# A hybrid decoder step on one core: side work placed by an estimated clock of each engine, weights split two pieces ahead

## The chip, the cores and the metric

The kernel runs on one core of a Trainium2 chip. The metric is the device time of one execution in microseconds; the median of several runs is given. In the text PE is TensorE, DVE is VectorE, ACT is ScalarE, POOL is GpSimd and SP is SyncE, which here only issues DMAs.

## What is computed

One layer of a decoder for 2048 prompt tokens and 8 sample tokens (one new token each for 8 sequences with a paged cache of 4096 positions), all in float32, with a model width of 1024. Cut to what matters:

```python
mod = silu(c) @ w_ada + b_ada                 # shift, scale and gate, twice
h = rmsnorm(x, norm1_g) * (1 + scale1) + shift1
z = h @ w_in
y_a = chunk_spatial_gating(gelu(z_a), ...)    # group A, 256 columns
y_b = silu(layernorm(causal_dwconv(glu(z_b), 31 taps)))   # group B, 256 columns
y_c = attend(q, k, v, logf)                   # group C, 8 heads x 64, forgetting attention
y = concat(rms(y_a), rms(y_b), rms(y_c)) * mix_g
x = x + gate1 * (y @ w_out)
h = rmsnorm(x, norm2_g) * (1 + scale2) + shift2
up = causal_dwconv(h @ w_up, 3 taps)          # d_ff = 2816
x = x + gate2 * ((silu(up[:, :d_ff]) * up[:, d_ff:]) @ w_down)
```

The sample tokens go through the same layer with the same weights. Their attention reads 32 pages of 128 positions for keys and as many for values, per sequence, through a page table. The results are the normalized outputs, the new K, V and forget rows, and the convolution states.

## The kernel before

**Stages.** The prompt is cut into 4 chunks of 512 tokens (`NCH`, `T`), each of 4 blocks of 128 (`NB`). Phase 1 (to about 670 us) makes norm1, the product with `w_in` and what hangs on it, chunk by chunk; phase 2 (to about 1180 us) is the prompt's attention; phase 3 is `w_out`, norm2, `w_up`, the short convolution, `w_down` and the final norm. The order in phase 3 is w_out of chunks 0 and 1, then per chunk four parts, each of an `up` (6 or 4 column tiles `j`) and a `down`. The w_out of chunks 2 and 3 stands before the last `down` of the chunk ahead of it. Each large product is done three times in a reduced float32 type: both operands are split in a high and a low part (`wh`, `wl`; `hh`, `hl`; `ah`, `al`; `yh`, `yl`), and `mm3` (lines 84 to 86) multiplies high by high, low by high and high by low. There are 9792 of these triples. The program's place is counted in them below: "product n".

**Weights.** `piece()` gives out weight pieces in a fixed sequence: `raw` is loaded by SP three pieces ahead, ACT copies it to `wh`, POOL subtracts for `wl`, one piece ahead of its use.

**Side work.** All that isn't one of the large products is written as Python generators, and fixed places in the main loops step them: `next(self.side)` behind groups of products (norm_c, norm2), `advance()` and `later(gen, delay)` in phase 1 with delays counted in groups, `ada_rest` with two steps a group in chunks 1 and 2, `bg(n)` for the sample attention, which hands out `n` credits that the yielded numbers use up. Each engine executes its own instructions in the order in which the program writes them, so these places decide who waits for whom. In phase 1 the ada weights (`wada`, four tiles for each of 8 steps of `k`, twice) are loaded through ACT's queue, and norm1 of the next chunk transposes 8 tiles of `x` at a time, then `modulate` makes `hmod`, `hh` (ACT) and `hl` (DVE).

**Sample attention** (lines 1100 to 1240). Per sequence s, `logits(s)` multiplies 16 tiles `pg` (two pages of keys each) by the query `qb`, sums to `red` and scales into `S`, all on DVE. `values(s)` takes the maximum `mx` on DVE, transposes it on PE, makes `dg`, spreads it with a product of ones, exponentiates on ACT, sums `lsum` and spreads that by PE, then makes the value products: each of 16 value tiles (two pages) gives two matmuls of 32 output columns, into the 32-row strip `j = 2 * (x % 2) + i` of `po`. A last one adds the new token (`vs`). The generators of one sequence's values and the next one's logits alternate. Value tiles come from `pg` and, while `lent` is set, from the buffers `yy` of w_out's `y` (named `yv` then), never more than 3 of each held. After the last sequence, `sample_rows` makes the sample tokens' gating, convolution and norms in 8 rows, and leaves them transposed in `hsT`, which w_out of the last chunk uses: `sample_mm` takes the `raw` weights of that w_out.

**w_out of chunks 2 and 3** reads `y` by pairs: `y_of` issues a load of `yh` and one of `yl` for up to three pairs ahead, on SP. `norm_c` normalizes group C of one chunk (`wk` holds squares and factors) in four steps with counts between (`waits`).

## Time and profile before

| what | value |
|---|---|
| median of 3 runs | 3123.56 us (3122.35 to 3125.27) |
| the profiled execution | 3115.85 us |
| its span | 3113.7 us, 41614 instructions |
| granted TensorE clock, mean | 0.975 of full |
| PE busy in 0 to 60, 60 to 670, 670 to 1180, 1180 to 3113 us | 38.6, 561.6, 489.5, 1861.9 us |
| granted clock in the same | 0.94, 0.97, 0.95, 0.98 |
| DMA | 523.9 MB, mean 168 GB/s |

How to read the rows that follow. A row of a group of instructions has its line, engine and operation, the tiles (output before the arrow, inputs behind) and their shapes, a count, the busy time and the mean of one in ns, and the idle time of the engine in front of it with what ended it. A row of PE's waits names the waiting instruction, what released it, and the sum, number and longest of the waits. The profile records two entries for a plain float32 matmul of the value strips.

### The profile page before, as it was taken

The page shows a single profiled execution, that of the slowest core. Times are in us where ns is not written, and L with a number is a line of the kernel's source. Part 1 is how long each engine was busy: PE and PEld are TensorE (multiplying, and loading weights), DVE is VectorE, ACT ScalarE, POOL GpSimd, SP SyncE. Part 2 cuts the span into 40 slices and gives each one's busy share as a digit, 9 for nine tenths or more (in the row PEclk, how much of TensorE's full clock was granted, in tenths as well). Part 3 has the DMA queues.
Part 4 walks back from the last instruction along what each step waited for, and adds up shares of the span by engine and source line. Part 5 has one row for each costly group of instructions (what it writes and reads, how often), then busy time and mean ns, then how long its engine had stood idle before and what let it go on. Part 6 is the DMA issues. An engine that isn't in the chain of part 4 may idle for free. (4 is left out here: it accounts for less than half of the span.)

```text
span 3113.7 us, 41614 instructions
## 1 busy us (share of the span) xinstructions
PE 2951.6 (95%) x14352; PEld 2151.2 (69%) x14352; DVE 2087.9 (67%) x2767; ACT 1228.0 (39%) x1717; POOL 1338.4 (43%) x884
## 2 busy tenths in 40 slices
PE   7998989899999989989999999999999999999998
PEld 4776768765555547767776767777767776777775
DVE  4838384858777763986887968785958554645454
ACT  4453535233333343434335433443433433534333
POOL 3544354423333444544444444454444454344443
PEclk9999999999999979999999999999999999999999
DMA  8355756563412327766677787678866627322222
GB/s 260 108 181 171 238 174 205 150 176 80 95 44 63 99 81 281 226 209 200 200 220 236 220 246 212 206 220 284 261 185 191 177 79 235 111 82 82 82 82 78
DMA packets 443589, 523.90 MB, mean 168 GB/s; under 512 B 35111, under 2 KB 281173, under 8 KB 443362
## 3 DMA queue, kind: packets, MB, share of 16 engines
q1 hardware_dynamic: 414418, 478.25, 51.3%
q10 hardware_dynamic: 28672, 41.95, 4.0%
q8 instruction: 113, 1.85, 0.2%
q0 software_dynamic: 288, 1.05, 0.1%
q14 instruction: 98, 0.80, 0.1%
HBM read 453.08 MB, written 68.38 MB: 167 GB/s over the span
## 5 line engine op out<-in xcount | busy, mean ns | idle before, releaser
L1525 POOL TENSOR_TENSOR wl<-raw,wh 128x1024 fp32r<-128x1024 f32 x296 | 769.3, 2609 | 874.9 <-ACT wh L1524 841.9
L84 PE MATMUL acc<-hh,wh 128*128 128x512 f32 x1792 | 721.0, 403 | 3.1 <-ACT hh L451 2.1
L85 PE MATMUL acc<-hl,wh 128*128 128x512 f32 x1792 | 709.4, 396 | 1.8 <-DVE hl L452 1.3
L86 PE MATMUL acc<-hh,wl 128*128 128x512 f32 x1792 | 709.1, 396 | 0.1
L1524 ACT CAST wh<-raw 128x1024 fp32r<-128x1024 f32 x296 | 308.8, 1047 | 552.9 <-PE acc L86 163.7
L1692 DVE SCALAR_TENSOR_TENSOR uy<-ub,fw,uy 128x512 f32<-128x512 f32 x352 | 282.8, 851 | 234.0 <-ACT uy L1689 232.6
L84 PEld LDWEIGHTS acc<-hh,wh 128*128 128x128 f32 x1792 | 338.2, 189 | 127.7 <-issue 22.0
L86 PEld LDWEIGHTS acc<-hh,wl 128*128 128x128 f32 x1792 | 338.4, 189 | 81.5 <-POOL wl L1525 1.0
L85 PEld LDWEIGHTS acc<-hl,wh 128*128 128x128 f32 x1792 | 338.6, 189 | 79.4 <-DVE hl L452 2.1
L496 POOL TENSOR_TENSOR wl<-raw,wh 128x512 fp32r<-128x512 f32 (+1 forms) x160 | 240.1, 1520 | 205.8 <-ACT wh L495 168.7
L84 PE MATMUL acc<-wh,ah 128*128 128x512 f32 x752 | 310.6, 413 | 16.0 <-ACT ah L1698 11.1
L86 PE MATMUL acc<-wh,al 128*128 128x512 f32 x752 | 303.6, 404 | 1.6 <-DVE al L1699 1.6
L85 PE MATMUL acc<-wl,ah 128*128 128x512 f32 x752 | 303.1, 403 | 1.0 <-POOL wl L1525 1.0
L963 POOL TENSOR_TENSOR lsum<-lsum,pt 128x512 f32<-128x512 f32 x96 | 141.0, 1469 | 203.8 <-PE misc L965 102.5
L676 DVE SCALAR_TENSOR_TENSOR cv<-glu,convw,cv 128x512 f32<-128x512 f32 x240 | 226.0, 1004 | 0.0
L1164 DVE TENSOR_TENSOR pg<-pg,qb 128x1024 f32<-128x1024 f32 x128 | 198.4, 1552 | 36.0 <-DMA pg<-in_cache_k 32.7
L995 ACT ACTIVATE pt<-acc 128x1024 f32<-128x1024 f32 (+2 forms) x144 | 126.9, 883 | 240.0 <-PE acc L993 182.5
L84 PEld LDWEIGHTS acc<-wh,ah 128*128 128x128 f32 x752 | 145.7, 194 | 77.1 <-issue 23.9
L84 PE MATMUL acc<-wh,hh 128*128 128x256 f32 (+2 forms) x552 | 163.4, 296 | 9.2 <-DVE nm L871 7.2
L86 PEld LDWEIGHTS acc<-wh,al 128*128 128x128 f32 x752 | 145.3, 193 | 37.9 <-DVE al L1699 3.9
L869 DVE TENSOR_REDUCE nm<-acc 128x1 f32<-128x1024 f32 (+1 forms) x128 | 121.5, 950 | 71.8 <-PE acc L864 71.1
L85 PEld LDWEIGHTS acc<-wl,ah 128*128 128x128 f32 x752 | 145.8, 194 | 32.8 <-POOL wl L1525 1.4
(382 smaller groups left out, 4836.9 us busy)
## 6 DMA issues: line engine op xcount, KB each, us to landing
raw<-in_w_up SPq DMA_DIRECT2D x176, 512.0 KB
pg<-in_cache_k SPq DMA_DIRECT2D x256, 256.0 KB
raw<-in_w_down SPq DMA_DIRECT2D x88, 512.0 KB
yv<-in_cache_v SPq DMA_DIRECT2D x138, 256.0 KB
raw<-in_w_in SPq DMA_DIRECT2D x132, 256.0 KB
pg<-in_cache_v SPq DMA_DIRECT2D x118, 256.0 KB
wada<-in_w_ada ACTq DMA_DIRECT2D x64, 256.0 KB
raw<-in_w_out SPq DMA_DIRECT2D x32, 512.0 KB
```

Source lines behind the costliest of these rows:

```text
L84: nc.tensor.matmul(out, lhsT=lh, rhs=rh, start=start, stop=False)
L85: nc.tensor.matmul(out, lhsT=lh, rhs=rl, start=False, stop=False)
L86: nc.tensor.matmul(out, lhsT=ll, rhs=rh, start=False, stop=stop)
L496: nc.gpsimd.tensor_tensor(out=wl[:, :, 0:n], in0=raw[:, :, 0:n], in1=f(wh[:, :, 0:n]), op=ALU.subtract)
L676: nc.vector.scalar_tensor_tensor(out=y[:, m, :], in0=glu[:, m, j:j + T], scalar=self.convw[:, m, j:j + 1], in1=y[:, m, :], op0=ALU.mult, o ...
L869: nc.vector.tensor_reduce(out=m1, in_=flat[:, 0:full], axis=AX.X, op=ALU.max, negate=True)
L963: e.tensor_tensor(out=lsum[:, i, off:], in0=lsum[:, i, off:], in1=pt[:, i, 0:T - off], op=ALU.add)
L995: nc.scalar.activation(out=pt[:, :, 0:w], in_=ps[:, :, 0:w], func=AF.Exp)
L1164: nc.vector.tensor_tensor(out=t, in0=t, in1=qs[s].unsqueeze(1).broadcast_to([P, 2, 512]), op=ALU.mult)
L1524: nc.scalar.copy(out=wh, in_=raw)
L1525: nc.gpsimd.tensor_tensor(out=wl, in0=raw, in1=f(wh), op=ALU.subtract)
L1692: nc.vector.scalar_tensor_tensor(out=y[:, i, :], in0=ub[:, i, s:s + T], scalar=self.fw[:, s, n:n + 1], in1=y[:, i, :], op0=ALU.mult, op1=A ...
```

## The change

- **An estimate beside the program.** Every engine handle is wrapped: `Engine` calls the real instruction and tells `Estimate.note`, which keeps a clock for PE, DVE, ACT, POOL, SP and one for the DMA. A cost formula for each engine gives the end of the instruction; `Ring` and `State` keep for each tile when it is written, read and free.
- **Generators yield what they need.** Instead of a count, a generator yields a list of tiles (or a function such as `acc_free`), with the engine that will use them. `ok` lets it go on when the estimate says that these are ready by the engine's own clock (PE's if none is named), plus 0.1. `tick`, `more`, `fill` and `advance` ask at the places where the steps stood, and at some new ones.
- **Sample attention** has one generator for all logits and one for all values. A K tile is taken when its page should be there and DVE's clock is under PE's plus 5. Value tiles are loaded up to three at a time, in `yy` buffers while `lent`, and all that are there are multiplied at once. `lent` spans other parts: it is set ahead of chunk 0's first `down` and of the last `down` of chunks 1 and 2, and reset ahead of part 2's `up`. `force` flushes the values that hold `yy` buffers, and ahead of chunk 3's w_out all that is left of the sample work.
- **Phase 1.** `wada` is loaded by SP. norm1 of the next chunk, `ada_rest`, the gating, convolution, log-sigmoid and layer norm steps go through the same test; what is left is forced at the chunk's end. Group B's layer norm reads an SBUF copy instead of PSUM (4 more ACT copies).
- **Weights.** `ahead(2)` splits two pieces ahead, and is called in `up` also behind the copy to `ub`.

The core of the diff:

```diff
+    def note(self, e, op, args, kw):
+        ...
+        if op.endswith("dma_start"):
+            size = max(x.nbytes() if callable(x.nbytes) else x.nbytes for x in outs)
+            self.t[e] = t + 0.4
+            self.t["dma"] = max(self.t["dma"], t) + size / 240e3
+            end = self.t["dma"] + 1.8
+        else:
+            end = t + self.cost(e, op, outs, ins)
+            self.t[e] = end
...
+    def cost(self, e, op, outs, ins):
+        n = max(free(x) for x in outs + ins[:1])
+        if e == "tensor":
+            if op == "transpose":
+                return 0.11
+            n = free(ins[1])
+            if "float32r" in str(ins[1].dtype):
+                return max(0.107, 0.0045 + 0.000445 * n)
+            return 4 * max(0.045, 0.00042 * n) * min(1.0, outs[0].shape[0] / 128)
+        if e == "vector":
+            if op == "reciprocal":
+                return 0.1 + 0.0066 * n
+            sb = [x for x in ins if "PSUM" not in str(x.space) and free(x) > 1]
+            return (0.14 + 0.00105 * n) * (1.2 if len(sb) > 1 else 1.0)
+        if e == "scalar":
+            return 0.19 + 0.00083 * n
+        return (1.0 if n < 64 else 0.15) + 0.0023 * n
...
+    def ok(self, need, e="tensor"):
+
+        return not isinstance(need, list) or self.nc.ready(need) <= max(self.nc.t["tensor"], self.nc.t[e]) + 0.1
...
+    def tick(self, n=1):
+
+        for _ in range(n):
+            if self.ok(self.need):
+                self.need = next(self.side, None)
...
             if n == 0:
                 hh, hl = self.hT
                 nxt = self.norm1(c + 1) if c + 1 < NCH else iter(())
                 if c == NCH - 1:
+                    for _ in ada:
+                        pass
...
             self.advance()
-            if n >= 2:
-                next(nxt, None)
-            if adas:
-                next(ada, None)
+            if n == 2:
+                self.later(nxt)
...
-                self.nc.scalar.dma_start(out=w, in_=self.I["w_ada"][k * P:(k + 1) * P, c0:c0 + 512])
+                self.nc.sync.dma_start(out=w, in_=self.I["w_ada"][k * P:(k + 1) * P, c0:c0 + 512])
...
+        def more_v(s):
+
+            while vq and vq[0][0] == s and len(self.vt) < 3 and (self.lent or not kq and not kt):
+                if self.lent:
+                    self.vy += 1
+                    t = self.pw.tile([P, 2, 512], F32, name="yv", tag="yy", bufs=3)
+                else:
+                    t = pgp.tile([P, 2, 512], F32, name="pg")
+                self.vt.append(load(t, cv, *vq.pop(0)))
...
+            po, x = None, 0
+            while x < NP // 2:
+                more_v(s)
+                yield [*self.vt, vs] if self.vt else None
+                if po is None:
+                    po = self.misc()
+                while self.vt:
+                    t, g = self.vt.pop(0), x // 2
...
+            if kn and self.ok(kn, "vector") and (self.force or self.nc.t["vector"] < self.nc.t["tensor"] + 5):
+                went = True
+                kn = next(ks, None)
...
                 elif last:
                     if c + 1 == NCH - 1:
+                        self.force = True
                         for _ in self.sample_units:
                             pass
                     self.w_out(c + 1)
...
-                if n == 0 and c < NCH - 1:
+                if c < NCH - 1 and n == (len(parts) - 1 if c else 0):
                     self.lent = True
-                if n == 2 and c:
-                    self.lent = False
...
     def piece(self):
 
+        self.ahead(2)
+        self.used += 1
+        return self.split[self.used - 1]
...
-        while len(self.split) < min(self.used + 2, n):
+        while len(self.split) < min(self.used + k, n):
```

How the change moves the work, at three places. In the changed kernel all instructions carry the line of the wrapper, L100.

On PE in phase 3, value matmuls (`yv` or `pg` are value tiles, `S` the weights of the softmax) among up's products. Before, a group of eight:

```order
L84 MATMUL acc<-hh,wh 128x512
L85 MATMUL acc<-hl,wh 128x512
L86 MATMUL acc<-hh,wl 128x512
L1205 MATMUL misc<-yv,S 32x512 x6
L1205 MATMUL misc<-pg,S 32x512 x2
```

With the change, a group between down's products:

```order
L100 MATMUL acc<-wh,ah 128x512
L100 MATMUL acc<-wl,ah 128x512
L100 MATMUL acc<-wh,al 128x512
L100 MATMUL misc<-yv,S 32x512 x6
L100 MATMUL acc<-wh,ah 128x512
```

A group has six value matmuls, of three tiles, instead of eight of four.

On SP (its DMA issues) at the end of the sample's row work; `zb_s`, `vl_s` and `st_s` are row tiles, `yy` the pairs of w_out's `y`. Before:

```order
L1258 DMA cb_s<-in_conv_b 8x256
L1260 DMA ys<-ysc_d 8x512
L1264 DMA rows<-in_state_ffn_conv 128x5x128
L1265 DMA rows<-in_state_ffn_conv 64x128
L1271 DMA out<-zb_s 8x256
L1272 DMA glu_d<-zb_s 8x256
L1276 DMA out<-vl_s 8x256
L1518 DMA raw<-in_w_down 128x2x512
L1283 DMA st_s<-glu_d 128x16
```

With the change, in w_out of chunk 3:

```order
L100 DMA cb_s<-in_conv_b 8x256
L100 DMA ys<-ysc_d 8x512
L100 DMA rows<-in_state_ffn_conv 128x5x128
L100 DMA rows<-in_state_ffn_conv 64x128
L100 DMA out<-zb_s 8x256
L100 DMA glu_d<-zb_s 8x256
L100 DMA out<-vl_s 8x256
L100 DMA yy<-yl_d 128x512
L100 DMA yy<-yh_d 128x512
L100 DMA st_s<-glu_d 128x16
```

The list that stood among weight loads of a `down` now stands between the high and the low half of a y pair; its beginning, with the store of `ysc_d` and the loads of `za_s`, follows that pair's `yy<-yh_d`.

On PE in phase 1, the transposes for the next chunk; `x` is the next chunk's normalized block, `wada` the ada weights. Before, at one of four such places within the chunk:

```order
L84 MATMUL acc<-hh,wh 128x512
L85 MATMUL acc<-hl,wh 128x512
L86 MATMUL acc<-hh,wl 128x512
L432 MATMUL acc<-ident,x 128x128 x8
L255 MATMUL misc<-wada,csT 32x512 x4
```

With the change, at the boundary ahead of chunk 2:

```order
L100 MATMUL acc<-hh,wl 128x512
L100 MATMUL acc<-ident,x 128x128 x16
L100 MATMUL misc<-wada,csT 32x512
L100 MATMUL acc<-ident,x 128x128 x8
L100 MATMUL misc<-wada,csT 32x512 x3
L100 MATMUL acc<-ident,x 128x128 x8
L100 MATMUL misc<-wada,csT 32x512
L100 MATMUL acc<-hh,wh 128x512
```

The 32 transposes that stood eight at a time between products now stand in one place, ahead of the chunk's first product.

## Rows read from the trace of the kernel before

**Rows 1.** The page's busy time of each engine, share of the span, instructions:
```profile
PE 2951.6 (95%) x14352; PEld 2151.2 (69%) x14352; DVE 2087.9 (67%) x2767; ACT 1228.0 (39%) x1717; POOL 1338.4 (43%) x884
```

**Rows 2.** Waits of PE: who waited for what, us in total, times, longest:
```profile
PE misc L255 <- DMA wada<-in_w_ada: 17.2, 5, 7.0
PE acc L84 <- ACT ah L1698: 11.1, 3, 7.2
PE misc L1191 <- DVE lsum L1188: 10.6, 2, 5.7
PE misc L1184 <- DVE dg L1181: 9.4, 4, 3.9
PE acc L1487 <- DVE wk L1481: 7.7, 3, 3.0
...
PE acc L432 <- ACT vt L590: 5.8, 2, 4.2
```

**Rows 3.** Phase 2's end: PE, PEld, DVE, ACT, POOL busy, PEclk, DMA share, GB/s:
```profile
1088.00:1171.00 83.00, 73.26 (x233) 36.68 (x235) 55.96 (x76) 33.78 (x39) 37.03 (x27) 0.75 0.24 86
```

**Rows 4.** Timeline of PE behind the `ah` wait: start, duration, engine, line, count:
```profile
1376.14 0.63 PE L84 MATMUL acc<-wh,ah 128*128 128x512 f32 x1
1376.57 0.63 PE L85 MATMUL acc<-wl,ah 128*128 128x512 f32 x1
```

**Rows 5.** Timeline of PE, a round of value matmuls and products behind it:
```profile
2083.32 1.06 PE L1205 MATMUL misc<-pg,S 128*32 128x512 f32 x8
2084.31 0.50 PE L84 MATMUL acc<-hh,wh 128*128 128x512 f32 x1
2084.65 0.39 PE L85 MATMUL acc<-hl,wh 128*128 128x512 f32 x1
2084.88 0.39 PE L86 MATMUL acc<-hh,wl 128*128 128x512 f32 x1
```

**Rows 6.** The chain of waits from 2284 to 2345 us: two rounds; a lone matmul:
```profile
2289.15 1.85 PE misc L1205 x16
...
2336.35 0.97 PE misc L1208 x2
```

**Rows 7.** Timeline of SP's DMA issues, first and last of the sample rows' list:
```profile
2465.64 0.31 SPq L1221 DMA_DIRECT2D ysc_d<-oo  x1
...
2482.52 0.35 SPq L1283 DMA_DIRECT2D st_s<-glu_d  x1
```

**Rows 8.** Timeline of DVE, the sample rows' chain from the convolution to `ys`:
```profile
2506.83 1.47 DVE L1293 TENSOR_TENSOR st_s<-st_s,cw_s 128x496 f32<-128x496 f32 x1
...
2532.49 2.82 DVE L1314 SCALAR_TENSOR_TENSOR ys<-ys,rs_y,mg_s 8x512 f32<-8x512 f32 x1 [2.86 <-POOL rs_y L79]
```

**Rows 9.** The page's costliest groups, the low part of a weight piece:
```profile
L1525 POOL TENSOR_TENSOR wl<-raw,wh 128x1024 fp32r<-128x1024 f32 x296 | 769.3, 2609 | 874.9 <-ACT wh L1524 841.9
```

**Rows 10.** Groups on ACT from 60 to 670 us, busy and mean ns, idle before:
```profile
L450 ACT ACTIVATE hmod<-acc,modT,s 128x512 f32<-128x512 f32 x24 | 18.3, 772 | 1.7 <-PE acc L432 1.4 <-ACT zs L515 0.3
...
L451 ACT CAST hh<-hmod 128x512 fp32r<-128x512 f32 x24 | 14.6, 615 | 0.3
```

**Rows 11.** Groups on DVE from 1180 to 2610 us:
```profile
L1692 DVE SCALAR_TENSOR_TENSOR uy<-ub,fw,uy 128x512 f32<-128x512 f32 x264 | 218.6, 885 | 113.1 <-ACT uy L1689 113.0
L1164 DVE TENSOR_TENSOR pg<-pg,qb 128x1024 f32<-128x1024 f32 x128 | 198.4, 1552 | 36.0 <-DMA pg<-in_cache_k 32.7 <-DMA yv<-in_cache_v 3.3
L1166 DVE TENSOR_REDUCE red<-pg 128x16 f32<-128x1024 f32 x128 | 154.5, 1211 | 1.1
L1168 DVE SCALAR_TENSOR_TENSOR S<-red,S 128x16 f32<-128x16 f32 x128 | 82.3, 646 | 1.0
L1699 DVE TENSOR_TENSOR al<-uy,ah 128x512 fp32r<-128x512 f32 x66 | 81.6, 1237 | 29.0 <-ACT ah L1698 28.9
...
L1695 DVE TENSOR_TENSOR uy<-uy 128x512 f32<-128x512 f32 x66 | 48.6, 736 | 6.6 <-ACT uy L1694 3.4
```

**Rows 12.** One line alone, the scaling into `S`: duration ns min/median/max, first and last start:
```profile
L1168 DVE SCALAR_TENSOR_TENSOR S<-red,S x128: 153/168/2416, 1260.3 to 2375.4; 128x16 f32<-128x16 f32 x128
```

More of the change, by code (lines that the diff above doesn't have):

```diff
@@ L39, in f, with is_ap, free, __init__ @@
     return ap.bitcast(F32)
+def is_ap(x):
+    return type(x).__name__ == "AP"
+def free(ap):
+    n = 1
+    for _, m in list(ap.ap)[1:]:
+        n *= m
+    return n
+class State:
+    def __init__(self, since):
+        self.since, self.w, self.r, self.last = since, [], [], since
+    def span(self, ap):
+        step = ap.ap[0][0] or 1
+        lo = ap.offset % step if step > 1 else ap.offset
+        return lo, lo + sum((m - 1) * abs(q) for q, m in list(ap.ap)[1:]) + 1
+    @staticmethod
+    def after(items, lo, hi, e="none"):
+        return max((t for a, b, t, by in items if a < hi and lo < b and by != e), default=0.0)
+    def put(self, items, lo, hi, t, e):
+        items[:] = [x for x in items if x[3] != e or not (lo <= x[0] and x[1] <= hi)][-24:] + [(lo, hi, t, e)]
+        self.last = max(self.last, t)
@@ new lines, with __init__, tile, free_at @@
+class Ring:
+    def __init__(self, pool, est, bufs):
+        self.pool, self.est, self.bufs, self.made = pool, est, bufs, {}
+    def tile(self, shape, dtype, **kw):
+        t = self.pool.tile(shape, dtype, **kw)
+        made = self.made.setdefault(kw.get("tag") or kw["name"], [])
+        n = kw.get("bufs") or self.bufs
+        made.append(State(made[-n].last if len(made) >= n else 0.0))
+        self.est.tiles[t.tensor.name] = made[-1]
+        return t
+    def free_at(self, tag, n):
+        made = self.made.get(tag, [])
+        return made[-n].last if len(made) >= n else 0.0
@@ L318, in phase1 @@
                 if c == NCH - 1:
+                    for _ in ada:
+                        pass
+                    self.tasks = [t for t in self.tasks if t[0] is not ada]
                     for name in ("hta", "pa", "px"):
@@ L358, in fill @@
         next(self.filler, None)
+        for t in list(self.tasks):
+            if isinstance(t[1], list) and self.ok(t[1], t[2]):
+                self.step(t)
         if self.taps:
@@ L395, in ada_rest, with square @@
                 ready.append(load(g, k))
-                yield
+                yield list(ready[0])
                 next(gen)
-                yield
-            yield
-            for _ in gen:
-                pass
-            yield
+            yield from gen
+    def square(self, x, out):
+        junk = self.junk.tile([P, D], BF16, name="junk", bufs=1)
+        self.nc.scalar.activation(out=junk, in_=x, func=AF.Square, accum_out=out)
     def norm1(self, c):
@@ L1005, in attend @@
             if kb >= 2:
-                for _ in range(2 if kb >= 6 else 1):
-                    next(self.side, None)
+                self.tick(2)
             if kb >= 3:
@@ L1024, in bg, with more @@
             self.credit -= n
+    def more(self):
+        for _ in range(2):
+            if self.ok(self.wait, "vector"):
+                self.wait = next(self.sample_units, None)
     def sample(self):
@@ L1428, in phase3 @@
                 last = n == len(parts) - 1 and c + 1 < NCH
+                if n == 2 and c:
+                    self.lent = False
                 if last and c:
-                    assert not self.held[False]
+                    self.force = True
+                    while self.vy:
+                        next(self.sample_units)
+                    self.force = False
                     self.w_out_start(c + 1)
@@ L1464, in phase3, with norm_c @@
             self.close(name)
-    def norm_c(self, c, tile, waits=(3, 4, 2, 1)):
+    def norm_c(self, c, tile):
         nc = self.nc
@@ L1473, in norm_c @@
         q, hi = tile(2), tile(3)
-        for _ in range(waits[0]):
-            yield
+        yield ys
         sq = q[:, 0, :]
@@ L1547, in y_pair @@
         return [t[:, i, :] for i in range(2)]
-    def page_tile(self, value):
-        for own in (False, True) if value and self.lent else (True,):
-            if self.held[own] < 3:
-                self.held[own] += 1
-                return own, (self.pg if own else self.pw).tile([P, 2, 512], F32, name="pg" if own else "yv", tag="pg" if own else "yy", bufs=4 if own else 3)
     def y_load(self, c, tiles):
@@ L1667, in up @@
                 self.flush()
-                next(self.side, None)
-                if i == 0 and (j != tiles[-1] or len(out) != len(tiles) - 1):
-                    self.bg(2 if c or j > 2 else 0)
+                self.tick()
+                if i == 0 and (c or j > 2):
+                    self.more()
             if c == NCH - 1:
```

315 lines of the change are left out of this document (188 added, 127 removed).

## The prediction

> **What bounds the kernel now.** I read the busy line of the page first, then the waits of PE, then what a matmul costs, then the other engines. PE is busy for 95% of the span, DVE for 67%, ACT and POOL for about 40% [rows 1]. PE is the bound, so a change pays only where it shortens PE's own work or a gap in front of it. The rest of the span, 3113.7 - 2951.6 = 162 us, is gaps. The rows I use [rows 2] name the causes that the change touches: the page of ada weights (17.2 us in 5 waits), `ah` (11.1), the sample attention's `lsum` and `dg` (10.6 and 9.4), `wk` of norm_c (7.7) and the `vt` in front of norm1's transposes (5.8). A gap costs a second time. After long ones the granted clock is at the lower of its two levels (1.2 of 2.4 GHz) for a while: from 1088 to 1171 us, with several gaps in it, it is 0.75 on average [rows 3], and behind the 7.2 us wait for `ah` a 512-column product starts 0.43 us after the last [rows 4], while at full clock it is 0.23 [rows 5]. Time spent at the lower level is thus 46% lost.
>
> I count places in the program by the three-pass products that PE has done, of the 9792 there are: product n of the projections. At 0.232 us each a weight piece of 24 lasts 5.6 us and an up tile of 48 lasts 11.1.
>
> **1. Value matmuls come in threes of tiles instead of fours.** A value tile makes two matmuls, each on a 32-column strip of PE; four different strips make a round. In the trace a round alone (8 records are 4 matmuls) lasts 2084.31 - 2083.32 = 0.99 us [rows 5], and two rounds in a row 1.85 [rows 6]: 0.86 a round and 0.13 for entering and leaving. A lone matmul lasts 0.97 [rows 6], so the round costs the same with one strip in it as with four. The new code takes at most three tiles at a time, six matmuls on strips 0, 1, 2, 3 and again two: two rounds for three quarters of the work. Counted in the order, before makes 40 runs with 74 rounds, the changed kernel 58 runs (35 of them of six) with 94. 20 x 0.86 + 18 x 0.13 = **+19.5 us**, all on PE. If the second, half filled round ran at half its price, it would be 35 x 0.43 = 15 less, +4.5; with every odd matmul at 0.97 it is at most +24. I take 19.5, since the lone matmul is the nearest row.
>
> The Trainium skill, TensorEngine Tiling (Array Packing), Key Properties, says that the tiles of the array run independently and that changing the tiling mode drains TensorE. This case agrees with the first (0.97 against 0.99) and shows some 0.13 us for the second; both speak against more and smaller groups, and a forecast by the rule alone would be this same term.
>
> **2. The end of the sample work.** Before, sample attention ends in the middle of chunk 2 and the sample's row work is spread over three parts. Now the last values are flushed directly ahead of w_out(3), and the row work falls into it. Two stalls follow.
> The first is on SP. In the changed order, the store `ysc_d` and all 30-odd small loads of the row work stand between the `yh` and the `yl` of one y pair. The trace has the same list: from the `ysc_d` store at 2465.64 to `st_s<-glu_d` at 2482.52 it keeps SP 16.9 us [rows 7]. PE reaches the products that need this `yl` 37 products (8.6 us) after the store. With 3 to 4 us for the store's operand and the landing, PE waits about 12 us (5 to 14). Before, the queue behind this list held only weights three pieces ahead.
> The second is the chain. Six row transposes stand at product 7924, the eight `ys` transposes at 7968, and PE has 44 products (10.2 us) between. In the trace the path from the `st_s` product on DVE at 2506.83 to the last `ys` scaling's end, 2532.49 + 2.82 = 2535.3, takes 28.5 us [rows 8], and needs two DRAM round trips. PE would wait 18 us; some of the chain was then queueing behind the up tiles' DVE work, so 8 to 18, taken 15.
> Behind `ys` in SP's new order come the four `raw<-in_w_out` loads, so the next weights have to be loaded and split (`wl` alone is 2.6 us [rows 9]) while nothing else is left for PE: another 3 to 10, taken 6. Sum **+33 us** (16 to 42). The small gap in front of the same transposes before is not worth more than a few microseconds of it.
>
> **3. Phase 1.** The ada weights move from ACT's queue, where their issue stands behind ACT's work, to SP, and each set of products waits until its tile should have landed. Of the 17.2 us some 3 remain, where three sets are forced out together at chunk 3's start. The `vt` wait (5.8) and smaller ones of that kind go, -9 together; the clock after them gives back 9 more, being 46% of some 20 us at the lower level. Against that, the next chunk's 32 transposes no longer come in four groups of 8 between products, but all at the chunk's boundary. There ACT makes `hmod` and `hh` for each of 8 k, 8 x (0.772 + 0.615) = 11.1 us [rows 10], against some 9 us of PE's transposes and ada products; with the accumulator ring in between I put 4 us on each of three boundaries (0 to 8). -14 - 9 - 9 + 12 = **-20 us** (-35 to -5).
>
> **4. Phase 2.** norm_c's three PE steps were at fixed places. Now the first stands 5 us behind its operand, the second well behind, the third is forced at the end. Two thirds of 7.7 us go, and part of the low clock of [rows 3], whose whole price is 83 x 0.25 / 0.5 x 0.46 = 19 us. **-8 us** (-15 to +3).
>
> **5. Logits and values by the clock of the estimate.** A K tile costs DVE 1.552 + 1.211 + 0.646 = 3.41 us, an up tile 4 x 0.885 + 0.736 + 1.237 = 5.51 [rows 11]. The estimate in the diff has 2.86 and 4.88. It fills an up tile of 11.1 us with 2.2 K tiles, where there is room for 1.6. In chunk 0 the K tiles at the start become fewer (16 against 20 by product 3312), which should dissolve the `ah` wait of [rows 2] with its low clock: **-10 us** (-20 to +10). In chunk 1, from product 4992 to 6000, the new order has 43 K tiles where there were 32. DVE gets 263 us of work (before 224) for 234 us of PE work, 29 us too much, and part of it ends as waits for `ah`, `mx` and `lsum`: **+12 us** (0 to +30). In chunk 2 fewer K tiles are left; the waits for `dg` and `lsum` there lose some 6 us, and norm2's blocks 2 and 3, now together at the last down part's half, take 4 back: **-2 us** (-10 to +8).
>
> **6. What costs nothing.** Splitting weights a half tile earlier lies under PE's work: ACT and POOL are idle more than half of the span [rows 1]. If the cover is gone, as in part 2, it is counted there. Four more copies of 1024 columns on ACT (about 1 us each) are hidden in phase 1.
>
> **Sum.** 19.5 + 33 - 20 - 8 - 10 + 12 - 2 = +24.5 us, on the profiled 3115.85 us: 3140. The median of the runs is 3123.56, 7.7 above; on that scale, 3148.
>
> **Rivals.**
> (a) Faster. The estimate is good enough that the waits of PE for DVE in phase 3 go: `ah`, `lsum` and `dg` are 31 us, and half of that again in clock, so -45 for part 5 as a whole; phase 1 gives 32 instead of 20 and phase 2 gives 15. With +19.5 for the value rounds and the tail at its low end of 16: 19.5 + 16 - 32 - 15 - 45 = -56, which is 3067; I name 3082, since one of the three gains will come only in part. It goes this way if the tail costs under 20 us and the K bursts cost nothing. For it: those waits all come from fixed places. Against it: in the changed order 10 such steps still stand within 25 products of the DVE instruction that they need, before it was 11. Chance 0.2.
> (b) No change: the tail costs half (16) and chunk 1 nothing. 24.5 - 17 - 12 = -4.5, about 3120. Chance 0.13.
> (c) Slower still. The logits' short scaling `S` varies from 153 to 2416 ns with a median of 168 [rows 12]; the estimate puts it near the median. In K bursts DVE then falls behind and stays behind up to the end of the K tiles. Another 30 us on part 5: 3178. Chance 0.17.
> The Trainium skill, GPSIMD Engine Reference, Key points, says that GpSimd shares its SBUF interfaces with VectorE, so that they contend. That fits the spread of `S` beside POOL's long `wl`, but no run here shows that it is the cause.
> The forecast itself, a net loss between the two, has 0.5.
>
> **How the numbers follow.** About 6 us (0.2%) can be told from no change. From the forecast's half, 0.44 is slower, 0.04 within and 0.02 faster; (a) is faster; of (b) 0.04 is faster and 0.06 the same, 0.03 slower; (c) is slower. Faster 0.26, same 0.10, slower 0.64. Eight in ten: without the lower half of (a) and the upper half of (c), 3082 to 3185.
>
> **What would show it.** Right: PE's waits name `yl` and `ys`, or `misc<-ident,ys` behind DVE, with over 10 us each near the last chunk's w_out; groups of 12 value records that take as long as 16; no ada wait over 3 us; three short gaps at transposes of `x` with ACT behind them. Wrong: a group of 12 records at 1.4 us; no gap over 5 us ahead of chunk 3; DVE's waits as long as before, or a wait for `ah` in chunk 1 over 20 us.

## The result and the profile after

The changed kernel takes 3193.12 us in the median (3190.43 to 3200.56, 4 runs), the kernel before 3122.95; the ratio is 1.0231 with a 95% interval of 1.0208 to 1.0254. The forecast was 3148, so the direction was right and the loss nearly three times as large: 70 us instead of 25. The profiled execution has 3190.99 us and a span of 3189.3, 75.6 above the span of before.

The page of the changed kernel, busy time of each engine and the granted clock in tenths of full speed by slices of the span, to be read against [rows 1]:

```profile
PE 2992.6 (94%) x14352; PEld 2160.8 (68%) x14352; DVE 2109.7 (66%) x2767; ACT 1231.4 (39%) x1721; POOL 1363.5 (43%) x884
...
PEclk9998999899999999999999999999999998999999
```

PE is busy 41.0 us longer, and its gaps grew by 75.6 - 41.0 = 34.6. Both traces were cut at the same places of the program. The count n of the texts above, up to 9792, is of single matmuls and not of triples: three of them make one product. The start of matmul n divides phase 1's chunks 0 to 2, chunk 3 with phase 2, then phase 3's chunk 0, chunk 1 and chunk 2 up to chunk 3's w_out, that w_out, and the rest. A single stretch can move by itself: 20 entries of ada products (7.8 us) that stood ahead of matmul 2016 stand behind it in the changed kernel, so the first two rows are best read together, +8.2 us against a forecast of -28. The last column is the whole time that PE spends on value matmuls, worked out from their starts:

| stretch (to matmul) | before | after | difference | forecast | of it value matmuls |
|---|---|---|---|---|---|
| phase 1, chunks 0 to 2 (2016) | 503.5 | 518.7 | +15.2 | -20 for phase 1 | |
| chunk 3 and phase 2 (2688) | 678.1 | 671.1 | -7.0 | -8 for phase 2 | |
| chunk 0 (4656) | 530.4 | 526.6 | -3.8 | -10 | +1.7 |
| chunk 1 (6288) | 430.1 | 447.4 | +17.3 | +12 | -2.0 |
| chunk 2 (7872) | 428.7 | 452.8 | +24.1 | -2 | +28.5 |
| w_out of chunk 3 (8064) | 50.0 | 77.7 | +27.7 | +33 | |
| the rest | 492.8 | 494.9 | +2.1 | 0 | |
| sum | 3113.7 | 3189.3 | +75.6 | +24.5, with 19.5 for values | +28.2 |

The same stretches in the changed kernel, with the busy time of PE, PEld, DVE, ACT and POOL, the granted clock, and the DMA's share and GB/s:

```profile
0.00:518.74 518.74, 452.66 (x2735) 356.95 (x2736) 298.55 (x478) 231.99 (x401) 236.31 (x159) 0.94 0.59 187
518.74:1189.84 671.10, 637.15 (x2834) 387.86 (x2834) 503.66 (x867) 240.92 (x343) 258.51 (x222) 0.98 0.39 103
...
1716.43:2163.83 447.40, 421.97 (x1781) 318.51 (x1781) 350.18 (x348) 162.44 (x197) 211.82 (x114) 0.96 0.68 212
2163.83:2616.66 452.83, 440.98 (x1902) 313.36 (x1900) 295.81 (x299) 174.78 (x222) 196.65 (x116) 0.98 0.66 199
2616.66:2694.36 77.70, 61.17 (x244) 40.60 (x243) 23.31 (x46) 20.53 (x32) 24.59 (x16) 0.82 0.59 176
```

The forecast missed at the first line: chunks 0 to 2 were to win, and lose, with a granted clock of 0.94. Of the 51.1 us between +24.5 and +75.6, phase 1 makes 35.2, the value rounds 8.7 and chunk 1 another 7.3; the other terms nearly cancel. The chunk with the value work and the last w_out lose about what was expected of them. The waits of PE in the changed kernel, to be read against [rows 2]:

```profile
PE acc L100 <- ACT ya L100: 18.6, 3, 8.1
PE acc L100 <- POOL vl L100: 17.9, 4, 7.5
PE acc L100 <- DVE t L100: 16.6, 5, 10.9
PE acc L100 <- ACT ah L100: 16.5, 3, 11.7
...
PE acc L100 <- POOL wl L100: 12.0, 7, 3.4
PE misc L100 <- DMA rows<-in_state_ffn_conv: 9.2, 1, 9.2
PE misc L100 <- DMA wada<-in_w_ada: 7.5, 4, 3.0
...
PE misc L100 <- DVE dg L100: 1.2, 1, 1.2
...
PE misc L100 <- DVE lsum L100: 0.2, 1, 0.2
```

What the change aims at did come: the sample's `lsum` and `dg` fell from 20.0 to 1.4 us, the ada page from 17.2 to 7.5. In their place stand `ya` and `vl` (36.5 us, group A's gating in phase 1), for which PE did not wait before, and `t` and `wl`, which were 3.5 and 1.7 us before.

**Where `ya` is lost.** DVE in the first chunk of the changed kernel, and the PE instruction that waits (start, duration, instruction, idle time before it):

```profile
110.65 1.21 DVE L100 TENSOR_TENSOR vl<-vl,bc 128x1024 f32<-128x1024 f32 x1
111.78 16.25 DVE L100 SCALAR_TENSOR_TENSOR cv<-glu,convw,cv 128x512 f32<-128x512 f32 x15
128.07 0.19 DVE L100 COPY glu<-halo 128x60 f32<-128x60 f32 x1
128.18 1.66 DVE L100 SCALAR_TENSOR_TENSOR ya<-acc,pv,za 128x256 f32<-128x256 f32 x4
```
```profile
134.24 2.53 PE L100 MATMUL acc<-ident,ya 128*128 128x128 f32 x8 [8.06 <-ACT ya L100]
```

Fifteen convolution taps (the `cv` rows, each one multiply-add of the 31-tap convolution) stand between `vl` and `ya`, 16.25 us. The program writes four of them there; the other eleven are written after `ya`. So the order in which the program writes DVE's work is not the order in which DVE gets it, against what the section on the kernel before says of each engine: when the program was built, taps that needed nothing were put ahead of `ya`, which needs a PE product. The estimate keeps its clock by the written order, so it had `ya` ready before PE reached the transposes, and PE stood 8.06 us, and 5.42 and 5.08 in the next two chunks. In the kernel before the same reordering stands in the trace (19 taps between the two in the first chunk), but there two groups of delay lay between: PE came to `vl` at matmul 480 and to `ya` at 576, and comes to them at 408 and 480 now.

### The profile page after: what moved, and what is told of

Same layout as the page of the kernel before. It is cut to its first block, busy times and chain, and to the rows that moved or that the text cites. A ratio compares the mean times of both kernels' runs of the same rounds, so it can differ in the third digit from the quotient of the medians.

```text
span 3189.3 us, 41636 instructions
## 1 busy us (share of the span) xinstructions
PE 2992.6 (94%) x14352; PEld 2160.8 (68%) x14352; DVE 2109.7 (66%) x2767; ACT 1231.4 (39%) x1721; POOL 1363.5 (43%) x884
## 3 DMA queue, kind: packets, MB, share of 16 engines
q8 instruction: 113, 1.85, 0.2%
## 4 chain that ended last, share of the span: by engine, by line
PE 63%; DVE 9%; issue 5%; POOL 3%; DMA 3%; ACT 2%; SPq 1%; POOLq 0%; ACTq 0%; DVEq 0%
PE acc L100 54%; PE misc L100 9%; POOL wl L100 2%; DVE pg L100 2%; DVE uy L100 1%; SPq L100 1%; DVE red L100 1%; DVE t L100 1%; DVE S L100 1%; DMA pg<-in_cache_k 1%; DVE lsum L100 0%; POOL rs L100 0%; ACT wh L100 0%; DVE xa L100 0%; DVE wk L100 0%
## 5 line engine op out<-in xcount | busy, mean ns | idle before, releaser
L100 POOL TENSOR_TENSOR wl<-raw,wh 128x1024 fp32r<-128x1024 f32 (+2 forms) x456 | 1031.7, 2275 | 1118.7 <-ACT wh L100 1053.3
L100 PE MATMUL acc<-hh,wh 128*128 128x512 f32 x1792 | 725.3, 405 | 8.4 <-ACT hh L100 6.9
L100 PE MATMUL acc<-hh,wl 128*128 128x512 f32 x1792 | 713.9, 399 | 8.1 <-POOL wl L100 8.1
L100 PE MATMUL acc<-hl,wh 128*128 128x512 f32 x1792 | 713.5, 398 | 3.5 <-DVE hl L100 3.5
L100 ACT CAST wh<-raw 128x1024 fp32r<-128x1024 f32 (+2 forms) x456 | 405.0, 895 | 660.4 <-PE acc L100 328.9
L100 DVE SCALAR_TENSOR_TENSOR uy<-ub,fw,uy 128x512 f32<-128x512 f32 x352 | 294.1, 883 | 250.8 <-ACT uy L100 249.1
L100 PEld LDWEIGHTS acc<-hh,wh 128*128 128x128 f32 x1792 | 340.8, 190 | 136.5 <-issue 26.5
L100 PEld LDWEIGHTS acc<-hh,wl 128*128 128x128 f32 x1792 | 340.7, 190 | 95.4 <-POOL wl L100 9.9
L100 PEld LDWEIGHTS acc<-hl,wh 128*128 128x128 f32 x1792 | 341.3, 190 | 84.2 <-DVE hl L100 5.2
L100 PE MATMUL acc<-wh,ah 128*128 128x512 f32 x752 | 308.5, 411 | 34.8 <-DVE t L100 16.6
L100 PE MATMUL acc<-wl,ah 128*128 128x512 f32 x752 | 302.1, 402 | 3.1 <-POOL wl L100 3.1
L100 PE MATMUL acc<-wh,al 128*128 128x512 f32 x752 | 302.0, 402 | 1.8 <-DVE al L100 1.7
L100 POOL TENSOR_TENSOR lsum<-lsum,pt 128x512 f32<-128x512 f32 x96 | 139.2, 1450 | 198.4 <-ACT pt L100 103.7
L100 DVE SCALAR_TENSOR_TENSOR cv<-glu,convw,cv 128x512 f32<-128x512 f32 x240 | 222.8, 992 | 0.0
L100 DVE TENSOR_TENSOR t<-acc,gate 128x1024 f32<-128x1024 f32 x80 | 97.5, 1219 | 182.4 <-PE acc L100 182.3
L100 DVE TENSOR_TENSOR pg<-pg,qb 128x1024 f32<-128x1024 f32 x128 | 189.3, 1482 | 35.8 <-DMA pg<-in_cache_k 35.5
L100 ACT ACTIVATE pt<-acc 128x1024 f32<-128x1024 f32 (+2 forms) x144 | 126.5, 882 | 222.8 <-PE acc L100 179.6
L100 PEld LDWEIGHTS acc<-wh,ah 128*128 128x128 f32 x752 | 144.2, 192 | 100.7 <-issue 30.3
L100 PEld LDWEIGHTS acc<-q,k 128*128 128x128 f32 (+1 forms) x640 | 106.6, 190 | 98.2 <-issue 39.3
L100 PE MATMUL acc<-q,k 128*128 128x512 f32 (+7 forms) x640 | 171.1, 390 | 1.1 <-DVE nm L100 1.0
L100 PE MATMUL acc<-k,q 66*128 66x512 f32 (+7 forms) x640 | 162.7, 375 | 10.0 <-DVE nm L100 7.9
L100 PEld LDWEIGHTS acc<-wh,al 128*128 128x128 f32 x752 | 144.5, 192 | 39.1 <-DVE al L100 3.7
```

Of the source, the lines that this page charges most:

```text
L100: res = f(*args, **kw)
```

## The experiments

Each run is the changed kernel with the edit shown, or with the edits that its expectation names; one is an edit of the kernel before. All ratios are to the kernel before, from runs beside it, with their 95% intervals.

**Value tiles two at a time.**

```diff
-                while self.vt:
+                for _ in range(min(2, len(self.vt))):
                     t, g = self.vt.pop(0), x // 2
```

(with the test that two are there, while more can be loaded)

> The changed kernel, with the value tiles multiplied two at a time (four matmuls, one round of strips) instead of three. Theory that a half filled round costs a full one: in the trace of the changed kernel the value matmuls take 101.4 us against 71.1 before; here they fall to 72 to 80 us, and the whole gets 20 to 28 us shorter. Rival, that the value matmuls are paid by their number and the rest was waiting for pages: they stay near 100 us, and the whole is the same within 6 us.

3173.10 us, 1.0163 (1.0138 to 1.0187): 20 us shorter than the changed kernel. PE's value work goes from 99.2 to 82.3 us, not quite to the 72 to 80 that were expected. The chains of waits of the changed kernel (a group of six, and a lone matmul) and of this one (a group of four):

```profile
2206.72 0.97 PE misc L100 x2
...
2320.01 1.84 PE misc L100 x12
```
```profile
2276.19 0.99 PE misc L100 x8
```

Six matmuls cost 1.84 us and four 0.99: the second, half filled round costs a full one. The Trainium skill, TensorEngine Tiling (Array Packing), Key Properties, has it that the array's tiles run independently of each other. For the value matmuls among themselves the rows agree: their time goes by how often the same strip is used, not by their number. The product `vs`, which ends each sequence, is another matter; it is taken up with part 1 below.

**Eight us more slack in phase 1's tests.**

```diff
-        return not isinstance(need, list) or self.nc.ready(need) <= max(
+        return not isinstance(need, list) or self.nc.ready(need) + self.margin <= max(
```

> The changed kernel, with each readiness test of phase 1 asking for 8 us more of slack. The theory is that the new waits of PE for vl and ya (17.9 and 18.6 us) are steps placed with no slack behind operands that are late in fact: they fall under 8 us together, and the whole gets 20 to 35 us shorter, since the lower clock after them goes too. Rival, that these operands are late by more than a few microseconds wherever they are placed, since ready convolution taps are always put in front of them: more than 20 us of the waits stay, and the whole gains under 10.

3183.67 us, 1.0192 (1.0171 to 1.0214), 9 us shorter than the changed kernel. The waits for `vl` and `ya` are gone from the first rows, and chunks 0 to 2 take 495.8 instead of 518.7 us. But chunk 3 and phase 2 take 688.1 instead of 671.1. PE's waits:

```profile
PE acc L100 <- POOL wl L100: 19.6, 11, 4.2
PE misc L100 <- DMA wada<-in_w_ada: 16.8, 6, 7.0
...
PE acc L100 <- ACT yb L100: 10.4, 1, 10.4
```

So the waits were steps with too little slack, as the first theory says, but the same slack for all steps delays others: `wada` is back at 16.8, and `yb` stands once for 10.4, behind the last product of phase 1, where what is left is forced. The expected gain of 20 to 35 did not come.

**DVE in written order, everywhere, in phase 1 only; and all four engines.** The wrapper queues each instruction behind the one written before it on its engine. The lines are those of the third run, in which `keep` holds up to the start of chunk 3; in the first it holds throughout, and in the second for all four engines:

```diff
-            res = f(*args, **kw)
+            with ExitStack() as order:
+                if self.name == "vector" and self.est.keep:
+                    if self.prev is not None:
+                        order.enter_context(self.est.tc.issue_after(self.prev))
+                res = f(*args, **kw)
+            self.prev = getattr(res, "ins", None) or self.prev
```

> The changed kernel, with DVE's instructions kept in the order in which the program writes them. In the built order of the changed kernel 15 convolution taps stand between vl and ya in the first chunk, where the program writes 4. Theory one, that the order in which DVE's queue is built undoes the estimate's placing: the waits for ya, t and ah (18.6, 16.6, 16.5 us) fall to under a third, and the whole gets 30 to 50 us shorter. Theory two, that the estimate's DVE prices are too low: the waits stay within a third of their size, the whole within 15 us.

> The changed kernel, with PE, DVE, ACT and POOL all kept in written order. Theory one (the built order undoes the placing): as with DVE alone or better, 40 to 70 us shorter, so about as fast as the kernel before. Theory two (prices too low): the waits of PE for DVE and POOL stay, and new ones come since nothing ready may go ahead: the same or longer by up to 40 us.

> The changed kernel, with DVE's written order kept in phase 1 up to the start of chunk 3 only. With it kept everywhere, the three chunks to product 2016 took 41.6 us less and the attention and chunk 0 of phase 3 lost 90. Theory that the built order of DVE causes the waits for vl and ya in phase 1: 30 to 45 us shorter than the changed kernel, with nothing given back later. Rival, that the gain is given back when chunk 3 and phase 2 start from there: under 15 us.

Everywhere: 3265.12 us, 1.0452 (1.0427 to 1.0476), 72 us longer than the changed kernel. With PE, ACT and POOL too: 3371.96, 1.0801 (1.0765 to 1.0837). As a theory of the whole, the first one falls: the waits for `ya` and `ah` went, but the built order (that in which an engine gets its work) does more good than harm in the attention and in chunk 0 of phase 3 (671.1 to 720.0 and 526.6 to 562.2 us with DVE alone). But in the three chunks for which it was drawn up it holds: 518.7 to 477.1. With the order kept there only, and everything else as in the changed kernel: 3147.46, 1.0087 (1.0070 to 1.0104), **46 us shorter**, 477.0 us for the three chunks and nothing given back (670.9 for the next stretch). DVE in the first chunk, and PE's waits from 40 to 480 us:

```profile
100.58 1.21 DVE L104 TENSOR_TENSOR vl<-vl,bc 128x1024 f32<-128x1024 f32 x1
101.71 6.95 DVE L104 SCALAR_TENSOR_TENSOR cv<-glu,convw,cv 128x512 f32<-128x512 f32 x4
112.90 1.66 DVE L104 SCALAR_TENSOR_TENSOR ya<-acc,pv,za 128x256 f32<-128x256 f32 x4 [4.24 <-PE acc L104]
```
```profile
PE misc L104 <- DMA wada<-in_w_ada: 8.3, 2, 4.3
PE misc L104 <- DVE lf L104: 7.8, 3, 2.7
```

Four taps stand in front of `ya`, which now waits for PE instead of PE for it, and neither `vl` nor `ya` is among the waits. The estimate's prices and the slack are the same in this run: the order is what brings these waits. Whether the kernel before would gain by the written order too was not run.

**The row loads from ACT.**

```diff
-            nc.sync.dma_start(out=st[pp, 0:CW - 1, :], in_=I["state_conv"][s]
+            nc.scalar.dma_start(out=st[pp, 0:CW - 1, :], in_=I["state_conv"][s]
```

(and the eight of `cw`)

> The changed kernel, with the 16 loads of the sample's convolution rows issued by ACT instead of SP. Theory that PE's 9.2 us wait for rows in chunk 3's w_out comes from SP's issues standing ahead of it: that wait falls by 6 us or more, since 16 issues of about 0.5 us leave SP. If the chain behind it (row norms to ys) is what sets the end, the wait for ys grows by as much and the whole changes by less than 5 us; if not, it is 6 to 14 us shorter.

3201.83 us, 1.0269 (1.0250 to 1.0288): 9 us longer than the changed kernel. PE's waits from 1150 us on:

```profile
PE misc L100 <- DVE ys L100: 14.7, 2, 13.6
...
PE misc L100 <- ACT sst L100: 5.4, 1, 5.4
...
PE misc L100 <- DMA rows<-in_state_ffn_conv: 2.6, 1, 2.6
```

The wait for `rows` falls from 9.2 to 2.6, so SP's list did cause it. The wait for `ys` rises from 5.1 to 14.7, since the row work on ACT stands behind the 16 issues, which hold it from 2618.4 to 2644.6 us. What sets the end is the chain to `ys`, and SP's list was only its first part. The expectation had the whole within 5 us for this case, so neither of its branches came as written.

**The earlier split alone, in the kernel before.**

```diff
             nc.gpsimd.tensor_copy(out=cu, in_=ub[:, :, T:])
+            self.ahead()
```

> The kernel before, with the one part of the change that splits weights half an up tile earlier (a call behind the copy to ub). Theory that it costs and brings nothing, since PE waited for weights 1.7 us in all: the same within 4 us. Rival, that the earlier split on ACT and POOL stands in front of uy and ah: 5 to 20 us longer, with more waits for ah.

3127.53 us, 1.0015 (1.0003 to 1.0028), 10 runs: some 5 us longer, between 1 and 9, so the loss of 70 doesn't come from it. Its profiled execution, the longest of the ten, shows how far one chunk can move with a small edit: chunk 1 of phase 3 takes 445.0 us instead of 430.1 there, with longer waits for `dg` and `mx`, and chunk 2 419.3 instead of 428.7.

**Three corrections together** (order in chunks 0 to 2, pairs, row loads on ACT).

> The changed kernel with three corrections at once: DVE's written order in chunks 0 to 2 of phase 1, value tiles two at a time, and the convolution rows' loads on ACT. If the three act at different places they add up: 40 + 20 + 0 to 10 us, so 3123 to 3135, at most 12 us above the kernel before. If they share a bound it stays above 3145.

3146.64 us, 1.0078 (1.0055 to 1.0100). No better than the first alone, though value work falls to 83.3 us. The loads on ACT cost 9 us here too (79.1 to 87.9 in chunk 3's w_out), and PE's gaps for `dg` came up to 10.7. The corrections did not add up.

**Longer use of the `yy` buffers, so that the sample work ends earlier** (on top of the order in chunks 0 to 2).

```diff
-                if n == 2 and c:
-                    self.lent = False
                 if last and c:
+                    self.lent = False
```

> The changed kernel with DVE's written order kept in chunks 0 to 2 of phase 1 (3147 us), and one more edit: value tiles may use the yy buffers through part 2 of chunks 1 and 2 too, so that sample attention ends 300 products earlier and the six row transposes stand at product 7752 instead of 7924, ahead of chunk 3's w_out. Theory that the 27 us in that w_out are paid for the row work falling into it: the stretch from product 7920 to 7968 goes back from 39.7 to about 12 us, and the whole gets 15 to 28 us shorter. Rival, that the rows' chain stalls PE wherever it stands: the gain is under 8 us.

3141.99 us, 1.0071 (1.0054 to 1.0088). From matmul 7920 to 7968 PE takes 12.4 us instead of 39.7, and the whole w_out 49.9, as in the kernel before (50.0). So the theory of the place holds: the 27 us are paid for the row work standing in that w_out. But only 5 us of it stay: chunk 1 takes 468.2 instead of 447.9, of which 14.0 are value work that moved there, and norm2's gaps behind w_out are 7 us longer. The 15 to 28 did not come.

**With pairs; with K tiles held; all together.** Held means that each K tile's multiply is queued on DVE behind what is written before it.

> The kernel with the longer use of the yy buffers, with value tiles two at a time besides. With the value work at about 80 instead of 100 us and the row work ended by product 7721: 35 to 50 us under 3147, so 3097 to 3112, which is faster than the kernel before by 10 to 25. If gaps at DVE take back what the value matmuls give, as in the run with three corrections, 3115 to 3130.

> The changed kernel with DVE's written order in chunks 0 to 2 of phase 1 (3147 us), and each K tile's multiply queued behind what the program writes ahead of it on DVE. Theory that the built order pulls K tiles forward in bursts, and that this makes the waits for ah (16.3) and t (16.0) in phase 3: both fall under 6 us and the whole gets 15 to 30 us shorter. Rival, that DVE is simply short of time in these stretches: the waits move to other names (h, lsum, dg) and the whole is within 8 us or longer.

> All four at once: DVE's written order in chunks 0 to 2 of phase 1, longer use of the yy buffers, value tiles two at a time, K tiles not pulled forward. If all four theories hold, 3147 - 20 (rows) - 20 (values) - 20 (K tiles), about 3087. If holding the K tiles brings nothing, as the run with longer buffers and pairs.

Held K tiles alone: 3148.79, 1.0091 (1.0074 to 1.0108), no change against 3147. The wait for `ah` falls from 16.3 to 3.5, but that for `t` goes from 16.0 to 19.5 and chunk 0 takes 12 us longer: the rival, that DVE is short of time there, fits better. The two others: 3195.02, 1.0253 (1.0224 to 1.0282), and 3193.43, 1.0242 (1.0222 to 1.0262), far off. A row of PE and one of SP say why, here from the first of them; the second has a wait of 85.9 us of the same kind:

```profile
2119.57 5.75 PE L104 MATMUL misc<-pg,S 128*32 128x512 f32 x10 [78.38 <-DMA pg<-in_cache_v]
```
```profile
2042.22 73.51 SPq L104 DMA_DIRECT2D pg<-in_cache_k  x60
```

PE stands 78 us for one value page, behind 60 loads of K pages. The flush ahead of w_out forces K tiles as well. As the program reads, each pass takes another K tile while the value tile isn't ready by the estimate, and the estimate's PE clock stands still. My edit let the flush begin in that state, so these two runs say nothing on their theories.

**The flush mended.** K tiles keep to their own test while only the value buffers are flushed:

```diff
-            if kn and self.ok(kn, "vector") and (self.force or self.nc.t["vector"] < self.nc.t["tensor"] + 5):
+            drain = self.force and not self.vy
+            if kn and self.ok(kn, "vector") and (drain or self.nc.t["vector"] < self.nc.t["tensor"] + 5):
```

> The kernel with the longer use of the yy buffers and value tiles two at a time, with one mend: while the values that hold yy buffers are flushed ahead of w_out, K tiles keep to their test (in the run before, 30 of them were pulled into the flush, and PE waited 78 us for a value page behind them). If the corrections to phase 1, to the value rounds and to the place of the row work are the whole of the loss, 3097 to 3115, at least 8 us under the kernel before. If what they free is taken by DVE and weight waits in chunks 1 and 2, 3118 to 3135.

> The same, with each K tile queued behind what the program writes ahead of it on DVE from chunk 1's part 2 on, the stretch (products 5520 to 7296) in which holding the K tiles took 12 us off. Theory that the K bursts there cost PE its waits for t and ah: 6 to 14 us under the run with the mend alone. Rival, that the longer use of the buffers has already spread them: the same within 4 us.

With the mend: **3112.80 us, 0.9967 (0.9955 to 0.9979)**, 10 runs: 80 us under the changed kernel and 10 under the kernel before, the one version here that beats both, and within the first of its two forecasts. Its stretches are 475.7, 670.9, 525.3, 447.6, 438.8, 50.9 and 503.2 us. Against the profiled execution before, which was 7.7 us under its median, it wins 40 in the first three and loses 39 in the other four. With K tiles held from chunk 1's part 2 on: 3132.98, 1.0038 (1.0023 to 1.0053), 20 us longer, 14 of them in chunk 2. So holding the K tiles is no remedy for what is left. PE's waits of the mended kernel:

```profile
PE acc L104 <- DVE nm L104: 15.3, 14, 4.2
PE acc L104 <- ACT ah L104: 11.7, 1, 11.7
PE acc L104 <- DVE h L104: 11.2, 6, 4.3
...
PE acc L104 <- DVE t L104: 8.6, 5, 3.3
...
PE acc L104 <- ACT wh L104: 7.1, 1, 7.1
...
PE acc L104 <- POOL wl L104: 5.6, 5, 1.8
```

## Why the prediction was right or wrong

**The value rounds (part 1): mechanism right, size too small.** +28.2 us on PE against 19.5. The 35 groups of six cost what the rows said (1.84 against 1.85). The term was mis-sized because I divided every other group by four and rounded up, and so put `vs`, which ends each of the eight sequences, into the round of the value matmuls in front of it. Five groups of two value matmuls and `vs` last 1.95 us, and three of one and `vs` 1.97, where I had counted one round of 0.99. That is 8 x 0.97 = 7.8 us, nearly all of the difference. In these groups no strip is used twice: the program writes `vs` on strip 0 and the last value tile on strips 2 and 3. One of them, the value matmul on strip 3, `vs`, and the product behind it:

```profile
2247.94 1.04 PE L100 MATMUL misc<-yv,S 128*32 128x512 f32 x2
2248.92 1.04 PE L100 MATMUL misc<-vs,S 1*32 1x512 f32 x2
2249.89 0.50 PE L100 MATMUL acc<-hh,wl 128*128 128x512 f32 x1
```

My upper end of 24 was too low for the same reason.

**The end of the sample work (part 2): right in place, +27.7 against +33, and near in size partly by luck.** The list on SP runs from 2619.45 to 2639.53, and PE waits 9.2 us where I had 12, though for `rows`, at the end of the list, and not for `yl`:

```profile
2619.45 0.28 SPq L100 DMA_DIRECT2D ysc_d<-oo  x1
...
2635.95 1.05 SPq L100 DMA_DIRECT2D rows<-in_state_ffn_conv  x2
...
2639.53 0.32 SPq L100 DMA_DIRECT2D st_s<-glu_d  x1
```

The chain from the `st_s` product to the last `ys` scaling, 28.5 us before [rows 8], takes 16.7 here:

```profile
2642.64 0.68 DVE L100 TENSOR_TENSOR st_s<-st_s,cw_s 128x496 f32<-128x496 f32 x1 [0.65 <-DMA st_s<-glu_d]
...
2658.61 0.74 DVE L100 SCALAR_TENSOR_TENSOR ys<-ys,rs_y,mg_s 8x512 f32<-8x512 f32 x1 [0.43 <-POOL rs_y L100]
```

DVE has little else to do in w_out, and of the 15 us of wait that I had taken for this chain 5.1 were left. So the two waits are 14.3 us, where I had 27, and the wait for weights (6) is not in the rows. What fills the gap I had not priced: at a granted clock of 0.82 in the stretch the matmuls that both kernels have there take 57.2 us instead of 50.0, and the transposes of the rows and a last sum of the sample attention, which stand there now, take 4.0. The experiments confirm the place (12.4 us for the 48 matmuls once the rows stand ahead of w_out) and the order of the two causes.

**Phase 1 (part 3): this step failed.** -20 forecast, +15.2 measured in chunks 0 to 2. The waits that I took away did go (`wada` 17.2 to 7.5, `vt` 5.8 to 1.2), and the boundaries with 32 transposes cost less than I had put on them: `hh` is 6.9 us in 4 waits in the whole run, none of them at the three boundaries. What I had left out is that the tests also bring group A's gating forward. In the text of the diff it stands as a changed yield; I took from the order only the steps that I had looked for, and did not compare where `vl` and `ya` stand on PE with how many taps stand ahead of them on DVE. With DVE's written order kept in these chunks the stretch takes 477.0 us, 26.5 under the kernel before, of which 7.8 are the ada products that moved behind it: the gain of 20 was there to be had, and the reordered queue made it a loss of 15.

**Phase 2 (part 4)**: -7.0 together with chunk 3, forecast -8. Right, and with the 7.8 us of ada products that came to this stretch better than forecast.

**Logits and values (part 5).** In chunk 1, +17.3 with 2.0 less value work, against +12: right in sign, and DVE is the busier for it (350.2 us, 328.2 before), but the waits are not the forecast `ah`, `mx` and `lsum`. The K tiles and `t` share DVE there, and PE's longest wait comes at its end:

```profile
2049.44 1.21 DVE L100 TENSOR_REDUCE red<-pg 128x16 f32<-128x1024 f32 x1
2050.57 2.29 DVE L100 TENSOR_TENSOR pg<-pg,qb 128x1024 f32<-128x1024 f32 x1
...
2059.36 2.42 DVE L100 TENSOR_TENSOR al<-uy,ah 128x512 fp32r<-128x512 f32 x1 [0.69 <-ACT ah L100]
2061.69 1.21 DVE L100 TENSOR_TENSOR t<-acc,gate 128x1024 f32<-128x1024 f32 x1
```
```profile
2062.96 0.79 PE L100 MATMUL acc<-wh,ah 128*128 128x512 f32 x1 [10.90 <-DVE t L100]
```

As much again, 11.4 us, PE waits in this chunk for weights (`wl` 9.8 in 5 waits, `wh` 1.6), where it waited for none before. At one place the copies `wh` stand on ACT behind the sample's exponential, which waits for DVE:

```profile
1966.36 0.45 ACT L100 ACTIVATE S<-S 128x288 f32<-128x288 f32 x1 [12.84 <-DVE S L100]
1966.71 1.99 ACT L100 CAST wh<-raw 128x1024 fp32r<-128x1024 f32 x2
```

No run shows what delays the weights elsewhere. In chunk 0 the `ah` wait was to dissolve; it grew (longest 7.2 to 11.7), and the 3.8 us gained come from elsewhere: the wait for `lsum`, 5.7 us before, is gone there. In chunk 2, without the value work, -4.4 against -2.

**The rest.** The split ahead costs little in the kernel before (part 6; some 5 us, between 1 and 9). That weights cost nothing was wrong all the same, as the 11.4 us of chunk 1 show; the sum had a term for them in the last w_out alone. Of the signs that I had named, the groups of 12 records and the ada waits came as said; waits of over 10 us in the last w_out and gaps at the transposes of `x` did not. Of the rivals, (c) gave the nearest time, but for another reason: it put the loss down to DVE's prices in the K bursts of phase 3. The loss in phase 1 goes with the order alone, at the same prices (477.0 us for chunks 0 to 2); whether better prices would help phase 3 was not run. The range failed at its upper end because phase 1 was bounded at -5: I had allowed for a smaller gain there and not for a loss.

What stays open is why the mended kernel is still above the kernel before in phase 3: by 17 us in chunk 1, 10 in chunk 2 and 10 in the rest. Part of it is value work (33.8 against 26.7 us in chunk 1, 30.6 against 22.7 in chunk 2). In chunk 1 the trace names most of the remainder: all of the `wh` wait of 7.1 us and 4.2 of the `wl` above lie there, and 4.2 for value pages. Holding K tiles made it no better, and no run shows why these come late.

## What to carry to other kernels

An estimate kept while a program is written knows only the written order. Where the queues are built in another order, compare the two engine by engine before trusting a step that has no slack, and pin the order (keep it as written) only where the trace shows that it hurts: pinned everywhere on DVE, it cost 72 us. Work that fills an array in rounds wants groups of whole rounds; count how often a strip is used, and count a product of another shape, as `vs` here, by itself. And look at what a test brings forward, not only at the waits that it removes.

## What was not expected of the hardware

The product `vs` takes 0.97 us of its own behind the value matmuls of another strip, 1.95 for the pair, while four value matmuls on four strips take 0.99 together. The two differ in that `vs` has operands of one row (`1*32` in the trace, against `128*32`); whether that is what keeps them apart no run here shows.

The granted clock averages 0.94 over the 519 us of phase 1 with the waits for `vl` and `ya`, against 0.97 in the same stretch before. The 2016 matmuls counted there take 358.4 us of PE's time instead of 349.6. With the order kept, at 0.97 and without these waits, they take 356.1, so how much of the difference is the price of the gaps in clock is not shown.
